# The first layer's output projection: one column block of four in seven block products for eight

## The chip, the cores and the metric

The kernel runs on one core of one Trainium2 chip. The metric is the device time of one execution in microseconds (us). Three runs of the kernel before took 1990.0, 1988.53 and 1989.0 us, with a median of 1989.0.

The engines are called by the profile's names: PE (TensorE, matrix products), PEld (its weight loads), DVE (VectorE), ACT (ScalarE), POOL (GpSimd), SP (SyncE, which here only issues DMAs).

## The reference

A trunk of two layers over 256 tokens of width 2048, in float32. What matters here is the first layer:

```python
n = rms_norm(h, attn_norm[i])
z = n @ a_w_in[j]
...
mix = neighbourhood_attention(q, k, v, a_rpb[j])
cross = memory_attention(qm, km, vm)
h = h + jnp.concatenate([mix, cross], axis=-1) @ w_o[i]
n = rms_norm(h, mlp_norm[i])
h = h + jnp.square(jax.nn.relu(n @ w_up[i])) @ w_down[i]
```

The change concerns the product with `w_o[0]`.

## The kernel before, in words

**Precision.** Each float32 operand of a product is split into a high part (rounded to the type that PE reads, `fp32r`) and a low part (the difference). A product is three matmuls: high by high, high by low, low by high, summed in PSUM. `split` (L506) makes the parts: a copy on ACT, then a subtraction on DVE.

**The attention output.** It lies in `cat` (L901 and after): 16 contraction tiles of 128 partitions, each with 256 high and 256 low columns, one column for each token. Head `hd` gives tile `hd`, the four memory heads the tiles 12 to 15. `attend3` (L682) writes a tile, the last one some five grains after the last key projection (`a_k_done`, L891).

**The output projection.** `add_o` (L1021) cuts the 2048 result columns into four blocks of 512, and each block's weights into four chunks of 1 MB (four contraction tiles by 512 columns). Blocks 0 and 1 are worked alternately, with the chunks in the order 3, 0, 1, 2, since the last heads are ready last; then block 2, then block 3, chunks 0 to 3 each. A chunk is a `Work` of two halves (`halves_of`, L252); a half is a "grain", the unit in which `run_all` (L446) walks through the program. A grain of the projection multiplies two contraction tiles: 2 tiles x 2 halves of the tokens x 3 matmuls, a 128x128 piece of `cat` as the stationary operand and 512 weight columns as the moving one (`m_products`, L379). Blocks 0 and 1 are grains 0 to 15, block 2 grains 16 to 23, block 3 grains 24 to 31.

**Ahead of a grain.** `ahead(n)` in `run_all` writes out, before grain n's products, the preparation of later ones: loads, "lift", "pre" and "prep", each by its own distance (`Grain`, L154). For the projection, "prep" issues the chunk's load on SP's queue into a ring of three places (`raw`, L274), and splits half a chunk into one of four places for high and low parts (`new_half`, L353; the split at L508 and L509). `later(n, ...)` puts a step n grains off. `past` (L933) makes a step come after a given pair of split instructions. The framework's planner then orders each engine's instructions by a modelled time and inserts the waits; an engine's queue runs in that order.

**PSUM.** Eight banks: four under the tag `acc`, which the sums of the blocks take by twos, two under `att`, and one pair `two` for the attention scores.

**After a block.** `o_done` (L939) adds a block's two sums to the residual `h` on DVE (L988) and sums squares on ACT (L922). After block 0 it also closes attention's scratch pool `work` and opens `side` in the same memory. After block 2, `guard` (L942) takes the mean square of three blocks as a provisional scale; blocks 0, 1 and 2 are scaled (L964), transposed in 32x32 blocks on DVE and by DMA (`far_blocks`, L620), and split into `hT` (`arrived`, L634; L538 and L539). Block 3 follows the same way (L1009). The true root mean square is put in later, by `inv` (L972). The MLP's first products (`up_grains`, L1055) read `hT`; three of them leave the last quarter of the contraction, which comes from block 3, for after one another's first three quarters (L1111).

**Where the method of the change already is.** The MLP's second product works on 2x2 blocks with seven products for eight. `down_grains` (L1176) copies a block of weights (L1198) and has POOL issue an accumulating DMA that adds another (L1199), adds three more sums on DVE (L1205 to L1207), and splits both parts; `squared` (L1133) makes the sums of the left operand. The lists `FIRST` and `SECOND` name each product with its left and right block:

```python
FIRST = ("p3", 6, 0), ("p1", 0, 1), ("p2", 2, 2)
SECOND = ("p7", 4, 0), ("p6", 5, 1), ("p4", 1, 2), ("p5", 3, 3)
```

p2, p3 and p4 go to one result block each; p1, p5, p6 and p7 are shared and folded by additions afterwards.

Of the kernel before, what the change touches and what calls it, by code (L numbers as in the profile page):

```python
# [10 lines left out]
F32 = mybir.dt.float32  # L11
# [6 lines left out]
P = 128  # L18
# [24 lines left out]
STEPPED = [sum(n for x, n in RUNS if x == q) for q in range(2)]  # L43

REST = (2, 0, 1, 3)
GUARD = 3

MOVING_AT = 160

# [101 lines left out]
class Grain:  # L151


    def __init__(self, run, after=None, load=None, pre=None, prep=None, ahead=(8, 5, 3), lift=None):  # L154
        self.run, self.after, self.stages = run, after, (load, lift, pre, prep)
        self.ahead = ahead[0], 8, *ahead[1:]


@with_exitstack
def encoder_kernel(ctx: ExitStack, tc: tile.TileContext, t: dict, out: bass.AP):  # L160
# [206 lines left out]
    def later(n, fn, *args):  # L367
        pending.append((state["tick"] + n, fn, args))
# [116 lines left out]
    def parts_of(name):  # L485

        return lambda k, i: tuple(box[name][:, k, b * SEQ + i * P : b * SEQ + (i + 1) * P] for b in range(2))
# [18 lines left out]
    def split(dst_hi, dst_lo, src):  # L506

        first = nc.scalar.activation(dst_hi, src, AF.Copy)  # L508
        return first, nc.vector.tensor_tensor(dst_lo, src, dst_hi.bitcast(F32), op=ALU.subtract)  # L509
# [40 lines left out]
    def summed(ps, name, row, factor=1.0):  # L550

        s = at.work.tile([P, SEQ], F32, tag="sum_s", name=f"{name}_s")
        nc.vector.scalar_tensor_tensor(s, ps, factor, row, op0=ALU.mult, op1=ALU.mult)
        return s
# [157 lines left out]
    def attention(jobs, at, gap=1, steps=(0, 1, 3, 4), rest=0):  # L712


        def step(n, job, prev):
            qT, kT, bias, v, head, cat = job
            if n == 0:
                res = attend(qT, kT, bias)
                box["scaled", head] = box["scaled"]
            elif n == 1 and len(steps) == 4:  # L720
                res = turned(prev)
            elif n < len(steps) - 1:
                res, box["pT", head] = halved(prev) if len(steps) == 4 else attend2(prev)
            else:
                if "between" not in box:
                    return attend3(prev, v, head, cat)
                with tc.issue_after(box.pop("between").ins):
                    return attend3(prev, v, head, cat)
            results[n, head] = res

        results = {}
        for t in range(len(jobs) + len(steps) - 1):
            for n in range(len(steps)):
                if 0 <= t - n < len(jobs):
                    j = t - n
                    more = rest if n == len(steps) - 1 and j == len(jobs) - 1 else 0
                    later(at + gap * j + steps[n] + more,
                          lambda n=n, job=jobs[j]: step(n, job, results.get((n - 1, job[4]))))
# [20 lines left out]
    def head_of(v, hd):  # L759
        return lambda part, kt: v[:, part, kt, hd * HD : (hd + 1) * HD]  # L760
# [130 lines left out]
    def a_k_done(hd):  # L891
        def f(w):
            k = at.work.tile([P, 512], F32R, tag="b_y2", name="kT")
            s = summed(w.ps, "k", box["x_row"])
            split(k[:, :SEQ], k[:, SEQ:], s)
            b = at.work.tile([P, (ROWS + 2) * GRID_W], F32, tag="b_o", bufs=3, name="bias")
            nc.sync.dma_start(b[:, : NT * NEAR], t["bias"][hd])
            attention([(box.pop(("q", hd)), k, b, head_of(box["v", hd // GH], hd % GH), hd, box["cat"])], 1)
        return f

    def a_qm_done(hd):  # L901
# [23 lines left out]
    def mean_square(which, n, name):  # L925

        s = small.tile([P, NT], F32, tag="ss0", name="ss_t")
        nc.vector.tensor_reduce(s, ssq[which][:, :, :n], axis=AX.X, op=ALU.add)
        v = keep.tile([P, NT], F32, tag=name, name=name)
        nc.vector.tensor_scalar(v, s, 1.0 / (n * 512), EPS, op0=ALU.mult, op1=ALU.add)  # L930
        return v
# [7 lines left out]
    def o_done(layer, nb):  # L939
        which = 2 * layer  # L940

        def guard():  # L942

            box["near"] = mean_square(which, GUARD, "near")
            box["scale"] = keep.tile([P, NT], F32, tag="scale", name="scale")
            nc.gpsimd.tensor_tensor(box["scale"], box["near"], mhalf[:, :NT], op=ALU.pow)
            box["hT"] = shifted(f"hT{layer}")

        def begun():

            y = at.side.tile([P, NT, 512], F32, tag="T", bufs=2, name="h_s")
            for i in range(NT):
                nc.scalar.activation(y[:, i, :], h[:, i, D - 512 :], AF.Copy, scale=box["scale"][:, i : i + 1])
            box["begun"] = y

        def scaled(b):

            if b < 2:
                box["room", b] = at.side.tile([P, 2, 1024], F32, tag="b", bufs=3, name="h_t")
                y = box["room", b][:, 0]  # L960
            else:
                y = at.side.tile([P, 1024], F32, tag="T", bufs=2, name="h_s")
            for i in range(NT):
                nc.scalar.activation(y[:, i * 512 : (i + 1) * 512], h[:, i, b * 512 : (b + 1) * 512], AF.Copy,  # L964
                                     scale=box["scale"][:, i : i + 1])
            box["raw", b] = far_blocks(lambda i: y[:, i * 512 : (i + 1) * 512], (box["room", b % 2][:, 1], y))
            box["still"] = y

        def landed(b):
            arrived(box["hT"], box["raw", b], b * 4, (G_M0, G_M1)[layer])  # L970

        def inv():  # L972

            v = mean_square(which, 4, "full")
            box["inv"] = keep.tile([P, NT], F32, tag="inv", name="inv")
            nc.vector.reciprocal(v, v)
            nc.vector.tensor_tensor(box["inv"], v, box["near"], op=ALU.mult)
            box["ninv"] = keep.tile([P, NT], F32, tag="ninv", name="ninv")
            nc.vector.tensor_scalar(box["ninv"], box["inv"], -1.0, None, op0=ALU.mult)

        def f(w):
            if nb == 0:
                closed("work")
                at.side = opened("side", side="right")
            def add():
                for i in range(NT):
                    hs = h[:, i, nb * 512 : (nb + 1) * 512]
                    added = nc.vector.tensor_tensor(hs, w.ps[i], hs, op=ALU.add)  # L988
                if nb == 0:
                    box["added"] = added  # L990

            def squares():
                for i in range(NT):
                    sum_squares(which, i, nb)

            if nb < 3:
                add()
                squares()
            if nb == GUARD - 1:
                later(1, guard)  # L1000
                for n, fn, *args in ((2, scaled, 0), (3, scaled, 1), (4, scaled, 2), (4, landed, 0), (5, landed, 1),
                                     (7, landed, 2), (7, begun)):

                    later(n, lambda fn=fn, args=args: past(lambda: fn(*args), box["weights"]))
            if nb == 3:
                y = box["begun"]

                def summed(i):
                    nc.vector.scalar_tensor_tensor(y[:, i, :], w.ps[i], box["scale"][:, i : i + 1], y[:, i, :],  # L1009
                                                   op0=ALU.mult, op1=ALU.add)  # L1010
                    return y[:, i, :]

                raw = far_blocks(summed, (box["still"], y.rearrange("p t c -> p (t c)")))
                box["summed"] = box["turned"]
                box["ready"] = arrived(box["hT"], raw, 12, (G_M0, G_M1)[layer])
                later(8, past, add)
                later(10, past, squares)
                later(12, lambda: past(inv, box["both", 1]))
        return f

    def add_o(layer):  # L1021
        first, second, third, late = 3, 0, 1, 2
        for n in (0, 2):
            if n:
                order = [(b, c) for b in range(2) for c in range(4)]
            else:
                order = [(b, c) for b in range(2) for c in (first, second)]
                order += [(b, c) for c in (third, late) for b in range(2)]
            add_ms([([t[f"w_o{layer}"][nb * 4 + c] for c in range(4)], o_done(layer, nb)) for nb in (n, n + 1)],
                   parts_of("cat"), order)  # L1030
            if layer and n == 0:
                plan[-1].behind = plan[-2].behind = plan[-1].last_block = True

# [830 lines left out]
```

## Time and profile before

| what | before |
|---|---|
| median of three runs | 1989.0 us (1988.53 to 1990.0) |
| the profiled execution | 1989.6 us |
| its span in the profile | 1987.8 us |
| granted clock of PE | 0.999 |
| DVE, ACT, POOL busy | 87%, 73%, 8% of the span |
| read from HBM | 397.78 MB, 202 GB/s over the span |

The span runs from the first to the last instruction on the chip; 1.8 us of the execution lie around it. A row of the timeline reads: start in the span, length, engine, line, operation, `out<-in`, the tile (for a matmul stationary x moving), the count, and in brackets how long the engine sat idle before it and what ended that. Matmuls are pipelined: the length of one is a latency, and the next one starts before it ends. PEld works beside PE. Busy times of a stretch are sums for each engine, so engines overlap in them.

### The profile page before, as it was taken

The page shows a single profiled execution, that of the slowest core. Times are in us where ns is not written, and L with a number is a line of the kernel's source. Part 1 is how long each engine was busy: PE and PEld are TensorE (multiplying, and loading weights), DVE is VectorE, ACT ScalarE, POOL GpSimd, SP SyncE. Part 2 cuts the span into 40 slices and gives each one's busy share as a digit, 9 for nine tenths or more (in the row PEclk, how much of TensorE's full clock was granted, in tenths as well). Part 3 has the DMA queues.
Part 4 walks back from the last instruction along what each step waited for, and adds up shares of the span by engine and source line. Part 5 has one row for each costly group of instructions (what it writes and reads, how often), then busy time and mean ns, then how long its engine had stood idle before and what let it go on. Part 6 is the DMA issues. An engine that isn't in the chain of part 4 may idle for free.

```text
span 1987.8 us, 33096 instructions
## 1 busy us (share of the span) xinstructions
PE 1977.8 (99%) x12816; PEld 1796.3 (90%) x12816; DVE 1729.1 (87%) x2098; ACT 1443.7 (73%) x2109; POOL 152.6 (8%) x205
## 2 busy tenths in 40 slices
PE   9999999999999999999999999999999999999998
PEld 8999999899999999999998888889999999999997
DVE  6777777589999999999999879789999999999997
ACT  6755555478887878777887657668788777877786
POOL 0000000000000000000001001001000000000001
PEclk9999999999999999999999999999999999999999
DMA  7856555768777777777778765668777777777775
GB/s 289 319 193 209 199 193 184 267 210 258 218 231 236 229 230 239 225 241 232 223 228 222 269 221 172 218 205 260 239 225 227 236 230 229 237 229 241 228 227 157
DMA packets 112862, 453.51 MB, mean 228 GB/s; under 512 B 19009, under 2 KB 42689, under 8 KB 65345
## 3 DMA queue, kind: packets, MB, share of 16 engines
q1 hardware_dynamic: 92320, 414.43, 61.1%
q0 software_dynamic: 20096, 36.45, 10.4%
q8 instruction: 100, 1.64, 0.3%
q10 hardware_dynamic: 288, 0.52, 0.1%
q14 instruction: 58, 0.47, 0.1%
HBM read 397.78 MB, written 4.19 MB: 202 GB/s over the span
## 4 chain that ended last, share of the span: by engine, by line
PE 98%; DVE 1%; issue 0%; DMA 0%; ACT 0%; SPq 0%; POOL 0%; DVEq 0%; POOLq 0%; ACTq 0%
PE ps_u L411 35%; PE ps_s L411 10%; PE p L1231 10%; PE p L1235 10%; PE p L1234 10%; PE ps_m L391 7%; PE ps_m L392 7%; PE ps_m L388 7%; DMA raw<-in_w_first 0%; PE sc_ps L605 0%; PE sc_ps L604 0%; PE sc_ps L606 0%; PE av L698 0%; PE av L699 0%; PE av L700 0%
## 5 line engine op out<-in xcount | busy, mean ns | idle before, releaser
L411 PE MATMUL ps_u<-hT,uh 128*128 128x256 f32 x3812 | 662.5, 276 | 0.0
L411 PEld LDWEIGHTS ps_u<-hT,uh 128*128 128x128 f32 x3812 | 578.7, 188 | 5.7
L411 PE MATMUL ps_u<-hT,ul 128*128 128x256 f32 x1964 | 542.6, 276 | 0.0
L508 ACT ACTIVATE uh<-raw_U 128x1024 fp32r<-128x1024 f32 x258 | 273.5, 1061 | 154.0 <-PE ps_u L411 151.6
L411 PEld LDWEIGHTS ps_u<-hT,ul 128*128 128x128 f32 x1964 | 368.7, 188 | 0.0
L508 ACT ACTIVATE hi<-raw 128x1024 fp32r<-128x1024 f32 (+1 forms) x215 | 222.1, 1037 | 183.0 <-PE ps_m L392 93.1
L509 DVE TENSOR_TENSOR lo<-raw,hi 128x1024 fp32r<-128x1024 f32 (+1 forms) x215 | 255.0, 1191 | 108.0 <-ACT hi L508 107.2
L509 DVE TENSOR_TENSOR ul<-raw_U,uh 128x1024 fp32r<-128x1024 f32 x258 | 314.2, 1219 | 9.2 <-ACT uh L508 9.2
L509 DVE TENSOR_TENSOR tl<-t,th 128x2048 fp32r<-128x2048 f32 x120 | 274.8, 2290 | 51.4 <-ACT th L508 51.1
L508 ACT ACTIVATE th<-t 128x2048 fp32r<-128x2048 f32 x120 | 231.0, 1925 | 91.3 <-PE p L1235 91.3
L509 DVE TENSOR_TENSOR bl<-b,bh 128x1536 fp32r<-128x1536 f32 x120 | 210.2, 1752 | 0.0
L1199 POOL DMA_DIRECT2D t<-b x120 | 104.4, 870 | 1156.9 <-ACT t L1198 1097.2
L1231 PE MATMUL p<-th,a_s 128*128 128x512 f32 x480 | 187.5, 391 | 0.0
L1234 PE MATMUL p<-tl,a_s 128*128 128x512 f32 x480 | 187.2, 390 | 0.0
L1235 PE MATMUL p<-th,a_s 128*128 128x512 f32 x480 | 186.7, 389 | 0.0
L508 ACT ACTIVATE bh<-b 128x1536 fp32r<-128x1536 f32 x120 | 178.8, 1490 | 3.5
L411 PE MATMUL ps_s<-nT,hi 128*128 128x256 f32 x896 | 154.6, 277 | 0.0
L1235 PE MATMUL p<-bh,a_s 128*128 128x512 f32 x360 | 140.9, 391 | 0.0
L1234 PE MATMUL p<-bl,a_s 128*128 128x512 f32 x360 | 140.1, 389 | 0.0
L1231 PE MATMUL p<-bh,a_s 128*128 128x512 f32 x360 | 140.1, 389 | 0.0
L411 PEld LDWEIGHTS ps_s<-nT,hi 128*128 128x128 f32 x896 | 135.3, 188 | 0.2
L411 PE MATMUL ps_s<-nT,lo 128*128 128x256 f32 x448 | 124.2, 277 | 0.0
(298 smaller groups left out, 3669.2 us busy)
## 6 DMA issues: line engine op xcount, KB each, us to landing
raw_U<-in_w_up SPq DMA_DIRECT2D x128, 1024.0 KB, 6.4
b<-in_w_pair SPq DMA_DIRECT2D x120, 1024.0 KB, 5.8
raw<-in_w_o SPq DMA_DIRECT2D x32, 1024.0 KB, 5.0
t<-b POOLq DMA_DIRECT2D x120, 256.0 KB, 6.6
raw<-in_w_b SPq DMA_DIRECT2D x21, 1024.0 KB, 5.4
raw<-in_w_av SPq DMA_DIRECT2D x12, 1024.0 KB, 5.0
raw<-in_w_aq SPq DMA_DIRECT2D x12, 1024.0 KB, 4.9
raw<-in_w_ak SPq DMA_DIRECT2D x12, 1024.0 KB, 4.8
```

The costliest lines, as they stand in the source:

```text
L388: first = nc.tensor.matmul(ps, ah, hi[:, s], start=st, stop=False)
L391: nc.tensor.matmul(ps, ah, lo[:, s], start=False, stop=False)
L392: final = nc.tensor.matmul(ps, al, hi[:, s], start=False, stop=sp)
L411: ins = nc.tensor.matmul(ps, x, acts[:, k, part], start=k == n == 0, stop=k == KT - 1 and n == 2)
L508: first = nc.scalar.activation(dst_hi, src, AF.Copy)
L509: return first, nc.vector.tensor_tensor(dst_lo, src, dst_hi.bitcast(F32), op=ALU.subtract)
L1199: nc.gpsimd.dma_start(s[:, 3, :], b[:, 1, :], accum_op=ALU.add)
L1231: ins = nc.tensor.matmul(ps, a[:, 0, ai, :], hi[:, s], start=entered, stop=False, skip_group_check=True)
L1234: nc.tensor.matmul(ps, a[:, 0, ai, :], lo[:, s], start=False, stop=False, skip_group_check=True)
L1235: nc.tensor.matmul(ps, a[:, 1, ai, :], hi[:, s], start=False, stop=ends, skip_group_check=True)
```

## The change

Block 2 of the first layer's projection (columns 1024 to 1535) is worked in another way for three of its four chunks, 3, 0 and 1; chunk 2 stays as it was and goes first. In each half of the three chunks, two contraction tiles, two halves of the tokens and two halves of the columns (256 each) make 2x2 blocks, and seven products of blocks take the place of eight: 21 matmuls over 256 columns for 12 over 512, in each of six grains. The grains keep their number and places.

- `sums_ahead`, called after the last key head, makes the sums of the left operand for six pairs of contraction tiles: ACT copies the high parts of `cat`, POOL issues an accumulating DMA of the low parts, DVE makes four sums, and they are split. They are spread over ticks 1 to 12. The scratch has two places in a tile of attention's pool; the results take the place of `nT`.
- `half(...)` prepares a grain: the load of a chunk (first of its two grains), an ACT copy of 256 columns with an accumulating DMA from POOL (two places, `s_x`), three DVE additions, and two splits, 768 columns into the ring's places and 1024 into `t_x` (three places).
- The sums lie in the two `att` banks and the pair `two`; block 3 takes `acc` as before.
- `fold` copies the shared sums out of PSUM, combines them by four subtractions of 256 columns, and adds all to `h`.
- The provisional scale of the first layer is taken from two blocks; the second layer's stays at three.
- The weights of the three chunks are reordered on the host: the four blocks of a half as 3, 0, 2, 1.

```diff
-GUARD = 3
+GUARDS = 2, 3
+CROSSED = (3, 0, 1)
+CROSSED_NB = 2
...
     def a_k_done(hd):
...
+            box["last_k"] = split(k[:, :SEQ], k[:, SEQ:], s)
...
+            if hd == NH - 1:
+                sums_ahead()
...
          def f(w):
...
-            if nb < 3:
+            if layer == 0 and nb == CROSSED_NB:
+                w.fold()
+                squares()
+            elif nb < 3:
                 add()
                 squares()
-            if nb == GUARD - 1:
+            if nb == 2:
                 later(1, guard)
...
+    def sums_ahead():
+        pairs = [4 * c + 2 * hf for c in CROSSED for hf in range(2)]
+        room = at.work.tile([P, 2, 8, P], F32, tag="l4", name="c_x")
+        box["crossed"] = keep.tile([P, len(pairs), 2, 4, P], F32R, tag="wide", name="a_x")
+        def together(n):
+            k, c = pairs[n], room[:, n % 2, :4].rearrange("p (k b) j -> p k (b j)", k=2)
+            both = box["cat"][:, k : k + 2, :].bitcast(F32)
+            nc.scalar.activation(c, both[:, :, :SEQ], AF.Copy)
+            nc.gpsimd.dma_start(c, both[:, :, SEQ:], accum_op=ALU.add)
+        def summed(n):
+            c, a = room[:, n % 2], box["crossed"][:, n]
+            nc.vector.tensor_tensor(c[:, 4, :], c[:, 0, :], c[:, 2, :], op=ALU.subtract)
+            nc.vector.tensor_tensor(c[:, 5:7, :], c[:, 0:8:4, :], c[:, None, 1, :].to_broadcast([P, 2, P]), op=ALU.add)
+            nc.vector.tensor_tensor(c[:, 7, :], c[:, 3, :], c[:, 6, :], op=ALU.subtract)
+            past(lambda: split(a[:, 0], a[:, 1], c[:, 4:]), box["last_k"])
+        for n in range(len(pairs)):
+            at_tick = max(2 * n, 1)
+            later(at_tick, together, n)
+            later(at_tick + 2, summed, n)
...
+        def fold():
+            z = at.side.tile([P, 4, SEQ], F32, tag="T", bufs=2, name="z_x")
+            hs = [h[:, i, nb * 512 : (nb + 1) * 512] for i in range(NT)]
+            for n in range(2):
+                nc.scalar.activation(z[:, 2 * n : 2 * n + 2].rearrange("p a b -> p (a b)"), sums["two"][:, n, :], AF.Copy)
+            for i in range(NT):
+                nc.vector.tensor_tensor(hs[i], sums["direct"][i], hs[i], op=ALU.add)
+            for d, x, y in ((1, 1, 0), (2, 1, 2), (1, 1, 3), (3, 3, 2)):
+                nc.vector.tensor_tensor(z[:, d], z[:, x], z[:, y], op=ALU.subtract)
+            for n, i in enumerate((1, 0)):
+                nc.vector.tensor_tensor(hs[i], z[:, 2 * n : 2 * n + 2].rearrange("p a b -> p (a b)"), hs[i], op=ALU.add)
+        def half(n, c, hf):
...
+            def lift():
+                b, s = blocks(), at.side.tile([P, 4, SEQ], F32, tag="T", bufs=2, name="s_x")
+                own["s"] = s
+                nc.scalar.activation(s[:, 3], b[:, 3], AF.Copy)
+                nc.gpsimd.dma_start(s[:, 3], b[:, 1], accum_op=ALU.add)
+            def pre():
+                b, s = blocks(), own["s"]
+                nc.vector.tensor_tensor(s[:, 0], b[:, 3], b[:, 0], op=ALU.add)
+                nc.vector.tensor_tensor(s[:, 1], s[:, 0], b[:, 1], op=ALU.add)
+                nc.vector.tensor_tensor(s[:, 2], s[:, 1], b[:, 2], op=ALU.add)
+            def prep():
+                own["b"] = [x[:, : 3 * SEQ] for x in new_half("M")]
+                box["weights"] = split(*own["b"], blocks()[:, :3].rearrange("p a b -> p (a b)"))
+                room = at.side.tile([P, 2, HALF], F32R, tag="b", bufs=3, name="t_x")
+                own["t"] = room[:, 0], room[:, 1]
+                split(*own["t"], own["s"].rearrange("p a b -> p (a b)"))
+            def run():
...
+                for products, (bh, bl) in ((FIRST, own["b"]), (SECOND, own["t"])):
+                    for name, ai, bi in products:
...
+                            own[name] = nc.tensor.matmul(ps, ah, bh[:, s], start=st, stop=False, skip_group_check=True)
+                        nc.tensor.matmul(ps, ah, bl[:, s], start=False, stop=False, skip_group_check=True)
+                        nc.tensor.matmul(ps, al, bh[:, s], start=False, stop=last, skip_group_check=True)
...
+            g = Grain(run, after, load if hf == 0 else None, pre, prep, lift=lift)
+            g.ahead = 6, 5, 4, 3
...
+            works = [([t[f"w_o{layer}"][nb * 4 + c] for c in range(4)], o_done(layer, nb)) for nb in (n, n + 1)]
+            if n and layer == 0:
+                crossed_works(o_done(0, CROSSED_NB))
+                works, order = works[1:], [(0, c) for c in range(4)]
```

## Prediction before the run

> **What bounds the kernel now.** I read the page first, then the tensor engine's rows in order of time around the first layer's output projection, then busy time by stage, and last the rows at the seam to the MLP.
>
> ```profile
> span 1987.8 us, 33096 instructions
> ## 1 busy us (share of the span) xinstructions
> PE 1977.8 (99%) x12816; PEld 1796.3 (90%) x12816; DVE 1729.1 (87%) x2098; ACT 1443.7 (73%) x2109; POOL 152.6 (8%) x205
> ...
> PE 98%; DVE 1%; issue 0%; DMA 0%; ACT 0%; SPq 0%; POOL 0%; DVEq 0%; POOLq 0%; ACTq 0%
> ```
>
> PE is busy for 99% of the span and makes up 98% of the chain that ended last. So work taken from PE is worth its full length, if PE stays fed. "Busy" is modelled, so I look at start times:
>
> ```profile
> 319.79 0.39 PE L411 MATMUL ps_s<-nT,hi 128*128 128x256 f32 x2
> ...
> 323.19 0.40 PE L411 MATMUL ps_s<-nT,hi 128*128 128x256 f32 x2
> ```
>
> ```profile
> 375.63 0.39 PE L388 MATMUL ps_m<-hi,cat 128*128 128x512 f32 x1
> ...
> 397.39 0.39 PE L388 MATMUL ps_m<-hi,cat 128*128 128x512 f32 x1
> ```
>
> Between the first two rows lie 30 matmuls over 256 columns (ten groups of two hi and one lo): 3.40 / 30 = 0.1133 us each. Between the second two lies the whole third block, 96 matmuls over 512 columns: 21.76 / 96 = 0.2267 us each. The "0.39" of a row is a latency; the spacing counts. Half the columns cost half the time to the last digit, although the narrow ones change their stationary tile every time too.
>
> ```profile
> 332.00:361.00 29.00, 29.00 (x134) 24.19 (x133) 17.44 (x26) 13.65 (x20) 0.00 (x0) 1.00 0.59 203
> 361.00:395.00 34.00, 34.00 (x152) 28.15 (x151) 20.18 (x19) 17.34 (x23) 0.00 (x0) 1.00 0.71 265
> 395.00:419.00 24.00, 24.00 (x108) 19.87 (x107) 19.15 (x26) 17.13 (x29) 0.71 (x1) 1.00 0.46 111
> ```
>
> Columns: stretch, length, then busy us of PE, weight load, DVE, ACT and POOL, the granted clock (1.00), DMA share. The stretches are blocks 0 and 1, the end of block 1 with block 2, and block 3. PE has no hole; DVE has 11.6, 13.8 and 4.9 us free, ACT 15.4, 16.7 and 6.9.
>
> **The change part by part.** *PE.* A pair of contraction tiles costs 2 tiles x 2 token halves x 3 = 12 matmuls of 512 columns, 12 x 0.2267 = 2.72 us (one grain). Seven products of 3 matmuls over 256 columns cost 21 x 0.1133 = 2.38 us. Six pairs save 6 x 0.34 = **2.04 us**, a tenth of a percent. The unchanged two grains run from 375.63 to 381.07, the six from there to 395.35, where block 2 ended at 397.39. No PE wait in the trace ends in this stage, so nothing else can be won here.
>
> The rows give no fixed cost of a matmul. [...]
>
> *Preparation of a grain.* Before: one ACT copy and one DVE subtraction over 1024 columns. After: an ACT copy of 256, an accumulating DMA from POOL, three DVE additions of 256, and two splits, of 768 and 1024.
>
> ```profile
> 382.36 1.23 DVE L509 TENSOR_TENSOR lo<-raw,hi 128x1024 fp32r<-128x1024 f32 x1 [1.49 <-ACT hi L508]
> ...
> 436.48 0.28 DVE L1149 TENSOR_TENSOR c<-c 128x128 f32<-128x128 f32 x1
> 436.80 0.42 DVE L1150 TENSOR_TENSOR c<-c 128x256 f32<-128x256 f32 x1
> ...
> 440.14 0.68 DVE L1205 TENSOR_TENSOR t<-b 128x512 f32<-128x512 f32 x1
> ```
>
> ```profile
> 328.72 0.40 ACT L508 ACTIVATE cat<-av_s 128x256 fp32r<-128x256 f32 x1
> ...
> 389.43 1.06 ACT L508 ACTIVATE hi<-raw 128x1024 fp32r<-128x1024 f32 x1 [1.66 <-PE ps_m L392]
> ```
>
> 768 columns lie between 512 and 1024: 0.95 us on DVE, and on ACT, between 256 and 1024, 0.85. DVE: 3 x 0.42 + 0.95 + 1.23 = 3.44 us a grain, ACT: 0.40 + 0.85 + 1.06 = 2.31, PE 2.38. So during the six grains **DVE is slower than PE**, by 6.4 us in all; only work done ahead can hide that. From 361 to two microseconds before the new end (393.35, the same end less 2.04) DVE would need 20.18 - 6 x 1.23 + 6 x 3.44 = 33.4 us of 32.35: 1.1 too many. ACT needs 17.34 - 6 x 1.06 + 6 x 2.31 = 24.8 and fits. What covers DVE is the lead of today's splits: the row at 382.36 ends at 383.59 and serves the grain that starts at 389.23 (five of 2.72 after 375.63), so 5.6 us can be eaten before PE feels it. If that cover were gone, the whole 1.1 would be PE's.
>
> *Sums of the left operand.* Six pairs, at ticks 1 to 12 after the last key head, so beside blocks 0 and 1: DVE 0.28 + 0.42 + 0.28 + 0.68 = 1.66, ACT two passes of 512, by the 256 and 1024 rows about 0.6 each. DVE takes 10.0 us of the 11.6 free in the first stretch, ACT 7.2 of 15.4: hidden, with 1.6 us to spare on DVE; without that, up to 10 us would be pushed into the stretch above. The accumulating DMA stands in POOL's queue behind the memsets of the last heads, which has cost nobody there, as the sums aren't read before 381.07.
>
> *The accumulating DMA and its two places.*
>
> ```profile
> raw<-in_w_o SPq DMA_DIRECT2D x32, 1024.0 KB, 5.0
> t<-b POOLq DMA_DIRECT2D x120, 256.0 KB, 6.6
> ```
>
> ```profile
> L1199 POOL DMA_DIRECT2D t<-b x120: 862/872/963, 431.8 to 1933.7; - x120
> ...
> DMA to landing us min/median/max: 3.2/6.6/10.8
> ```
>
> No 128 KB accumulation is in the trace; the same operation at 256 KB lands after 3.2 to 10.8 us. The sum tiles `s_x` have two places, their splits `t_x` three. The tightest chain I find is that of the sixth grain: `t_x` of the fourth needs the place of the first (free at 381.07 + 2.38 = 383.45), its split takes 1.06 + 1.23 = 2.29, then the sixth may be copied (0.40), issued (0.87), landed (L) and split (2.29): ready at 389.30 + L. PE reads it in the second half of that grain, 381.07 + 5 x 2.38 + 9 x 0.1133 = 393.99. So L up to 4.7 us is free; 6.6 makes PE late by 1.9, 10.8 by 6.1. Half the bytes should lie between the fastest and the median row; I take 5.0, **0.3 us late**. The weight loads on SP stay sixteen of the same size, now asked for some grains earlier:
>
> ```profile
> 355.84 0.33 SPq L274 DMA_DIRECT2D raw<-in_w_o  x1
> ```
>
> That place in the ring of three now takes the first changed chunk: landed at 355.84 + 5.0 = 360.8, twenty microseconds before use. Nothing else on SP waits for it.
>
> *Fold and seam.* At block 2's end come two ACT copies out of PSUM, four DVE subtractions of 256 and two more additions of 512: DVE 4 x 0.42 + 2 x 0.68 = 3.04 us beyond before, in block 3's stretch with 4.9 free, of which 1.8 are left.
>
> ```profile
> 418.84 1.69 DVE L539 SCALAR_TENSOR_TENSOR hT<-h_s,first,hT 128x256 fp32r<-128x256 f32 x4 [1.28 <-ACT hT L538]
> 420.44 0.75 DVE L1009 SCALAR_TENSOR_TENSOR h_s<-ps_m,scale,h_s 128x512 f32<-128x512 f32 x1
> ...
> 429.86 1.67 DVE L539 SCALAR_TENSOR_TENSOR hT<-h_s,first,hT 128x256 fp32r<-128x256 f32 x4
> ```
>
> ```profile
> 431.31 0.30 PEld L411 LDWEIGHTS ps_u<-hT,uh 128*128 128x128 f32 x2
> ```
>
> The last quarter of `hT` is started by DVE at 420.44, its first tile is split at 429.86 + 1.67 / 4 = 430.3, and PE reads it at 431.31: 1.0 us of slack. A backlog of DVE beyond 1.8 + 1.0 = 2.8 us reaches PE here. The guard helps: it sums two blocks now, so scaling of the first two need not wait for block 2. Backlog by the terms above runs from 1.1 to 5.6 us (the lead that may be eaten), late by 0 to 2.8; I take **0.9**, nearer to the low end.
>
> *Sum.* -2.04 + 0.3 + 0.9 = -0.8 us. The profiled execution took 1989.6 (span 1987.8 and 1.8 around it); it becomes 1988.8. The median of the runs is 0.6 lower, 1989.0, so the forecast in its terms is 1988.2.
>
> **The rivals.** *Full gain.* Every accumulation lands within 4.7 us and the seam keeps its slack: 1989.0 - 2.04 = 1987.0. For it: the 3.2 us row and PE's unbroken rate. Against: DVE is 99% booked from 332 to 393 (17.44 + 10.0 + 33.4 = 60.8 of 61.35).
>
> *DVE and the two places become the bound: slower.* `s_x` and `t_x` lie in the room that attention leaves, and the sums' scratch now lives there until the last of them. Two pairs go at a time: copy 0.6, issue 0.87, landing, sums 0.98, split 1.3. From 332, with 5.0 us of landing, three rounds of 8.8 end at 358, ahead of the first chunk; with 10.8, three of 14.6 end at 376. If the first copy comes only at 374, three rounds of 0.40 + 0.87 + 5.0 + 2.29 = 8.6 end at 399.8 instead of 393.99, 5.8 late, and the seam adds 0.9 to 2.8: 1989.0 - 2.04 + 7.6 = 1994.6. It decides from a first copy at about 373 on: then PE has lost over 6 us. Against it: POOL's 120 issues never took over 0.96 us, and DMA has room (share 0.59) in that stretch.
>
> *The gain is not there.* Were a narrow matmul held up by its weight load (0.19 us a row, overlapped), seven products would cost what eight did: 1989.0 plus the 1.2 of stalls, 1990.2. The 0.1133 spacing speaks against it, and the operands here have the same shapes.
>
> **How the numbers follow.** Forecast, with stalls up to 3 us: 0.45; full gain 0.25; slower rival 0.2; no gain 0.1. "Within 0.2%" is 1985.0 to 1993.0, about what a measurement of this kernel can tell from no change. Even a full gain stays inside, so faster gets 0.04, for a better order elsewhere; slower 0.21, the rival and some ends of the unknown landing. The range runs from full gain less the spread of the runs shown (1 us), 1986.0, to the latest landing, 1989.0 - 2.04 + 6.1 + 0.9 = 1994.0, which leaves out the worse half of the rival.
>
> **What would show it.** Right: narrow matmuls 0.113 apart in block 2, its end near 395.7, the stage from 361 nearly full on DVE, and the last `hT` read within a microsecond of its split. Wrong: holes in PE's starts before the fifth or sixth grain (landing over 4.7 us), a first `s_x` copy after 370, a spacing over 0.12, or PE waiting at the first MLP products for longer than 3 us.

## The result and the profile after

The changed kernel takes 1999.35 us, the median of six runs (1998.51 to 2000.78), beside 1989.27 us (1988.53 to 1990.0) for the kernel before in as many runs. The ratio is 1.0052 with a 95% interval of 1.0039 to 1.0065: **slower by half a percent**, 10 us. The forecast of 1988.2 us and its range up to 1994.0 us are both missed.

The head of the page of the changed kernel:

```profile
span 1998.2 us, 33317 instructions
...
PE 1980.2 (99%) x12870; PEld 1800.5 (90%) x12870; DVE 1749.9 (88%) x2152; ACT 1457.5 (73%) x2135; POOL 164.4 (8%) x217
...
PE 95%; DVE 2%; DMA 1%; ACT 1%; issue 1%; SPq 0%; DVEq 0%; POOL 0%; POOLq 0%; ACTq 0%
```

The span grew by 10.4 us, PE's busy time by 2.4. So most of the loss is not work: PE's share of the chain that ended last fell from 98% to 95%, and DVE, DMA, ACT and issue took what it left. The view of what PE waited for says where. The columns are the waiting instruction, what released it, the total in us, how often, and the longest. First the changed kernel, then the kernel before:

```profile
PE ps_u L415 <- ACT hT L542: 5.1, 2, 3.7
PE ps_u L415 <- DVE hT L543: 2.1, 1, 2.1
```

```profile
PE idle L240 <- POOL mhalf L234: 1.0, 1, 1.0
```

The longest before was the microsecond on `mhalf` at the kernel's start, which both have. New are 7.2 us on `hT`, the left operand of the MLP's first product. PE's rows in order of time, the changed kernel:

```profile
383.20 0.28 PE L1128 MATMUL ps_m<-hi,a_x 128*128 128x256 f32 x1
...
385.70 0.28 PE L1128 MATMUL ps_m<-hi,a_x 128*128 128x256 f32 x1
...
417.61 0.40 PE L415 MATMUL ps_u<-hT,uh 128*128 128x256 f32 x2
...
436.55 0.38 PE L415 MATMUL ps_u<-hT,uh 128*128 128x256 f32 x1 [3.73 <-ACT hT L542]
439.03 0.58 PE L415 MATMUL ps_u<-hT,uh 128*128 128x256 f32 x1 [2.10 <-DVE hT L543]
...
441.02 0.41 PE L415 MATMUL ps_u<-hT,uh 128*128 128x256 f32 x1
...
443.58 0.41 PE L415 MATMUL ps_u<-hT,uh 128*128 128x256 f32 x1
...
451.42 0.40 PE L1357 MATMUL p<-bh,a_s 128*128 128x512 f32 x1
```

and the kernel before:

```profile
419.15 0.40 PE L411 MATMUL ps_u<-hT,uh 128*128 128x256 f32 x2
...
441.10 0.40 PE L1231 MATMUL p<-bh,a_s 128*128 128x512 f32 x1
```

The projection ends 1.54 us earlier (417.61 for 419.15). From there to the first matmul of the MLP's second product lie 33.81 us (451.42 - 417.61) where there were 21.95 (441.10 - 419.15): 11.86 us lost, 10.3 in all. **Everything is gained inside the projection and lost at the seam behind it.** Busy time by stretch in the changed kernel; the columns are those of the prediction:

```profile
361.00:395.00 34.00, 34.00 (x199) 30.21 (x198) 29.87 (x44) 23.76 (x35) 6.41 (x7) 1.00 0.80 269
395.00:419.00 24.00, 24.00 (x125) 20.40 (x124) 23.30 (x32) 16.57 (x28) 0.00 (x0) 1.00 0.58 178
419.00:430.00 11.00, 8.75 (x75) 8.36 (x74) 7.19 (x9) 4.56 (x7) 0.00 (x0) 1.00 0.43 80
430.00:440.00 10.00, 4.18 (x30) 3.78 (x30) 4.99 (x8) 4.43 (x8) 0.86 (x1) 0.89 0.98 388
440.00:445.00 5.00, 5.00 (x26) 4.96 (x25) 1.97 (x4) 1.31 (x4) 0.00 (x0) 0.53 1.00 347
```

PE is full to 419. From 419 to 440 it stands still for 2.25 + 5.82 = 8.1 us, and in the last row the granted clock is 0.53. There 12 matmuls take 2.56 us (441.02 to 443.58), 0.213 each where 0.1133 is usual. Counted from start to start, the four holes are 1.67, 1.13, 4.00 and 2.48 us long; less one usual spacing each they cost 8.8. The 26 matmuls from 439.03 to 444.79 lie too far apart and cost another 2.8. Together that is 11.6 of the 11.9. In the ten microseconds from 430, where PE stands longest, DVE is busy for 4.99 and ACT for 4.43: what PE waits for is not a shortage of an engine but something that comes late. Followed back, it is one chain. The changed kernel, ACT's and DVE's rows:

```profile
405.57 0.45 DVE L1079 TENSOR_TENSOR z_x<-z_x 128x256 f32<-128x256 f32 x1
...
412.92 0.68 DVE L1081 TENSOR_TENSOR first<-z_x,first 128x512 f32<-128x512 f32 x1
...
415.06 2.09 DVE L631 STREAM_TRANSPOSE h_t<-h_s 128x512 f32<-128x512 f32 x2
...
422.02 1.71 ACT L542 ACTIVATE hT<-h_s,first 128x256 fp32r<-128x256 f32 x4 [5.19 <-DMA h_s<-h_t]
422.56 1.69 DVE L543 SCALAR_TENSOR_TENSOR hT<-h_s,first,hT 128x256 fp32r<-128x256 f32 x4 [3.93 <-ACT hT L542]
424.28 2.13 DVE L631 STREAM_TRANSPOSE h_s<-h_s 128x512 f32<-128x512 f32 x2
```

The kernel before, the same steps:

```profile
397.10 1.28 DVE L988 TENSOR_TENSOR first<-ps_m,first 128x512 f32<-128x512 f32 x2
...
410.06 2.09 DVE L627 STREAM_TRANSPOSE h_t<-h_s 128x512 f32<-128x512 f32 x2 [1.15 <-DMA h_t<-h_t]
...
418.29 1.71 ACT L538 ACTIVATE hT<-h_s,first 128x256 fp32r<-128x256 f32 x4 [2.76 <-DMA h_s<-h_t]
...
421.22 1.09 DVE L627 STREAM_TRANSPOSE h_s<-h_s 128x512 f32<-128x512 f32 x1
```

Block 2's last sum ends at 413.6 (412.92 + 0.68) instead of 398.4. The fold's subtractions and additions are strewn over eight microseconds, between splits and `hT` tiles in DVE's queue. So block 2 is transposed 5.0 us later (415.06 for 410.06) and the third quarter of `hT` split 3.7 later (422.02 for 418.29). And block 3's transposition writes into the room from which that third quarter is read (`box["still"]`, in `far_blocks`' second argument): it can't start before 424.25 and comes 3.1 us later (424.28 for 421.22). Then SP's queue and ACT's. The changed kernel:

```profile
426.44 1.27 SPq L634 DMA_DIRECT2D h_s<-h_s  x2
427.75 0.60 SPq L1178 DMA_DIRECT2D raw_U<-in_w_up  x1
428.39 1.27 SPq L634 DMA_DIRECT2D h_s<-h_s  x2
...
434.09 2.00 ACT L512 ACTIVATE u_z<-raw_U 128x1024 fp32r<-128x1024 f32 x2 [7.51 <-DMA raw_U<-in_w_up]
436.00 1.69 ACT L542 ACTIVATE hT<-h_s,first 128x256 fp32r<-128x256 f32 x4
```

The kernel before:

```profile
424.13 2.60 SPq L630 DMA_DIRECT2D h_s<-h_s  x4
426.78 0.61 SPq L1052 DMA_DIRECT2D raw_U<-in_w_up  x1
...
429.23 1.71 ACT L538 ACTIVATE hT<-h_s,first 128x256 fp32r<-128x256 f32 x4 [4.28 <-DMA h_s<-h_s]
...
432.50 2.02 ACT L508 ACTIVATE u_z<-raw_U 128x1024 fp32r<-128x1024 f32 x2 [0.72 <-DMA raw_U<-in_w_up]
```

**Two queues have changed their order.** Before, SP issued the four pieces of block 3's transposition and then the load `raw_U` of 1 MB; now the load stands between the second and the third piece. Before, ACT split the last quarter of `hT` and then `u_z`; now `u_z` stands ahead and waits 7.51 us for that very load. The last quarter, issued 2.3 us later (426.44 for 424.13), is split 6.8 us later (436.00 for 429.23). None of the lines that changed touches this load or this split.

### The profile page after: what moved, and what is told of

Its sections match the earlier page's. It is cut to its first block, busy times and chain, and to the rows that moved or that the text cites. A ratio compares the mean times of both kernels' runs of the same rounds, so it can differ in the third digit from the quotient of the medians.

```text
span 1998.2 us, 33317 instructions
## 1 busy us (share of the span) xinstructions
PE 1980.2 (99%) x12870; PEld 1800.5 (90%) x12870; DVE 1749.9 (88%) x2152; ACT 1457.5 (73%) x2135; POOL 164.4 (8%) x217
## 4 chain that ended last, share of the span: by engine, by line
PE 95%; DVE 2%; DMA 1%; ACT 1%; issue 1%; SPq 0%; DVEq 0%; POOL 0%; POOLq 0%; ACTq 0%
PE ps_u L415 34%; PE p L1357 10%; PE p L1361 10%; PE p L1360 10%; PE ps_s L415 9%; PE ps_m L395 7%; PE ps_m L396 7%; PE ps_m L392 7%; DMA first<-in_x 0%; DVE nT L543 0%; DMA h_s<-h_s 0%; SPq L634 0%; DVE hT L543 0%; PE sc_ps L608 0%; PE sc_ps L610 0%
## 5 line engine op out<-in xcount | busy, mean ns | idle before, releaser
L512 ACT ACTIVATE hi<-raw 128x1024 fp32r<-128x1024 f32 (+2 forms) x215 | 220.5, 1031 | 157.1 <-PE ps_m L396 72.3
L513 DVE TENSOR_TENSOR lo<-raw,hi 128x1024 fp32r<-128x1024 f32 (+2 forms) x215 | 253.2, 1183 | 80.6 <-ACT hi L512 80.0
L513 DVE TENSOR_TENSOR ul<-raw_U,uh 128x1024 fp32r<-128x1024 f32 x258 | 314.5, 1220 | 10.4 <-ACT uh L512 10.4
```

## The experiments

The theories go by letters. **F**: the fold makes block 2's last sum late. **P**: the preparation of the six grains (DVE's load, the accumulating DMAs) does. **G**: the guard over two blocks is itself the harm. **Q**: the changed order of the two queues carries the loss. **A**: the spacing of the narrow matmuls (0.119 us, below) comes from where their operands lie.

**Taking the fold out, and putting it on the kernel before.** The first kernel drops the fold's copies, subtractions and last additions:

```diff
         def fold():
-            z = at.side.tile([P, 4, SEQ], F32, tag="T", bufs=2, name="z_x")
...
-            for n in range(2):
-                nc.scalar.activation(z[:, 2 * n : 2 * n + 2]..., sums["two"][:, n, :], AF.Copy)
             for i in range(NT):
                 nc.vector.tensor_tensor(hs[i], sums["direct"][i], hs[i], op=ALU.add)
-            for d, x, y in ((1, 1, 0), (2, 1, 2), (1, 1, 3), (3, 3, 2)):
-                nc.vector.tensor_tensor(z[:, d], z[:, x], z[:, y], op=ALU.subtract)
-            for n, i in enumerate((1, 0)):
-                nc.vector.tensor_tensor(hs[i], z[...], hs[i], op=ALU.add)
```

> The changed kernel without the shared sums: p1, p5, p6 and p7 are computed but never copied out of PSUM nor added to the residual, so block 2 lacks them; the two direct additions stay. Theory F (the fold's eight extra operations, strewn over a booked DVE queue, hold up block 2's last sum, and through it hT): the last sum comes some 9 us earlier, hT no longer holds PE, 1987 to 1989 us. Theory P (the sixth grain's operand, prepared late in two places, ends block 2 at 401.3 instead of 395.4, and that alone makes hT late): block 2 still ends near 401, PE still waits, 1993 us or more.

Measured: 1990.4 us (1988.3 to 1992.35), ratio 1.0007 (0.9996 to 1.0018): the loss is all but gone, though the time lies a little above what F had, with the whole preparation in place, and the four pieces are issued together again. Block 2's products end even later there: the last one starts at 403.05, in the changed kernel at 401.28. The second is the kernel before with the fold's ten operations (two copies, four subtractions, two more additions beside its two) behind its plain block 2:

```diff
+            if layer == 0 and nb == 2:
+                z = at.side.tile([P, 4, SEQ], F32, tag="T", bufs=2, name="z_x")
...
+                for n in range(2):
+                    nc.scalar.activation(z[...], w.ps[n], AF.Copy)
+                add()
+                for d, x, y in ((1, 1, 0), (2, 1, 2), (1, 1, 3), (3, 3, 2)):
+                    nc.vector.tensor_tensor(z[:, d], z[:, x], z[:, y], op=ALU.subtract)
+                for n, i in enumerate((1, 0)):
+                    nc.vector.tensor_tensor(hs[i], z[...], hs[i], op=ALU.add)
+                squares()
```

> The kernel before with only the fold's operations added at the end of its plain block 2 (two ACT copies of its sums, four DVE subtractions of 256, two more additions of 512; they change block 2's values). No product, no preparation and no guard of the change. F: the block ends at 397.4 as before, but its last sum comes up to 10 us later and PE waits for hT: 1994 to 1999 us. P: a block that ends on time leaves room for the fold: 1989 to 1990.5 us.

Measured: 1999.86 us (1999.36 to 2000.14), ratio 1.0052 (1.0029 to 1.0075). **The fold alone costs as much as the whole change**, without one narrow matmul and without preparation (its guard is over three blocks still, of which more below). Its rows:

```profile
402.13 0.68 DVE L1005 TENSOR_TENSOR first<-z_x,first 128x512 f32<-128x512 f32 x1
...
426.76 1.27 SPq L630 DMA_DIRECT2D h_s<-h_s  x2
428.08 0.60 SPq L1063 DMA_DIRECT2D raw_U<-in_w_up  x1
...
434.07 2.00 ACT L508 ACTIVATE u_z<-raw_U 128x1024 fp32r<-128x1024 f32 x2 [7.19 <-DMA raw_U<-in_w_up]
435.98 1.69 ACT L538 ACTIVATE hT<-h_s,first 128x256 fp32r<-128x256 f32 x4
```

Here the last sum ends only 4.4 us later (402.13 + 0.68 for 397.10 + 1.28), and the same two orders have turned. So P is not needed for the turn: it comes without the preparation, and with the preparation but no fold it stays away.

**Less preparation, and the guard as it was.** One chunk of the three is kept in the new form, so two grains are prepared for six; and the guard is set back to three blocks:

```diff
-CROSSED = (3, 0, 1)
+CROSSED = (3,)
```

> The changed kernel with one chunk of three in seven products (two grains, 6 matmuls of 256 columns fewer, 0.68 us), so that the preparation is light and its two places do; fold and guard as in the change. F: the fold is whole, so most of the loss stays: 1994 us or more. P: block 2 ends on time, 1988 to 1990 us.

```diff
-GUARDS = 2, 3
+GUARDS = 3, 3
```

> The changed kernel with the provisional scale taken from three blocks again. F and P: scaling blocks 0 and 1 now waits for the late block 2 as well, so it is no faster than the change: 1999 us or more. A third theory G (the early scale lets transposes and splits of blocks 0 and 1 go ahead of the fold on DVE): the fold goes first, 1990 to 1996 us.

Measured: two grains 1999.34 us (1998.81 to 1999.67), ratio 1.0051 (1.0032 to 1.0071), no better than six. With the guard of three 2006.18 us (2005.66 to 2006.69, two runs), ratio 1.0083 (1.0054 to 1.0113): the early guard is worth 6.8 us (2006.18 - 1999.35), and G falls. It also sets the comparison above right. With a guard of three blocks in both, the change costs 6.3 us more than the fold alone (2006.18 - 1999.86). So the rest of the change is not free, the early guard pays for it, and that the two medians near 1999.5 agree is partly chance. The kernel with two grains tells more than its time:

```profile
424.50 1.93 SPq L634 DMA_DIRECT2D h_s<-h_s  x3
426.52 0.55 SPq L1178 DMA_DIRECT2D raw_U<-in_w_up  x1
427.12 0.61 SPq L634 DMA_DIRECT2D h_s<-h_s  x1
```

Its pieces begin at 424.50, 0.4 us later than in the kernel before, and still ACT splits the last quarter of `hT` only at 435.51, 6.3 us later than 429.23. One piece of four behind the load is enough. That speaks for Q over a mere lateness.

**The fold earlier.** The six new grains go first and the plain chunk last, in two banks of its own, so that the fold may run beside the plain chunk's products:

```diff
-        for n, c in enumerate(plain):
-            plan.append(Work("M", ..., begin, lambda w: None))
...
         plan.extend(half(2 * n + hf, c, hf) for n, c in enumerate(CROSSED) for hf in range(2))
+        for n, c in enumerate(plain):
+            plan.append(Work("M", ..., plain_begin, plain_done if n == len(plain) - 1 else None))
```

> The changed kernel with the six grains first and the plain chunk last, in banks of its own: the shared sums and the direct ones are folded while the plain chunk runs (one DVE addition of 512 more in all), so that only two additions stand behind block 2's end, as before the change. Theory F (the fold behind block 2 is what makes hT late, its length alone counts): 1987 to 1990 us. Theory Q (the fold is only the push: what costs is that the planner, its modelled times moved, lets a weight load stand between the pieces of block 3's transposition on SP, and the fourth weight column's split, which waits for that load, ahead of hT's last quarter on ACT): the built queues have that order here too, 1993 us or more.

Measured: 1999.23 us (1998.32 to 2000.13, two runs), ratio 1.005 (1.003 to 1.007). Nothing gained: the load still stands between the pieces. But the fold did not come early either. In DVE's queue its last addition starts at 409.74, and block 2's last sum ends at 414.7 (413.6 in the changed kernel). What F needed did not come about, so this run does not decide between F and Q.

**Holding the orders.** In the changed kernel the load of the MLP's fourth weight block is told to follow the last piece of the transposition (and is written out two grains later, 6 for 8 ahead), and the splits of that block to follow `hT`'s:

```diff
-            nc.sync.dma_start(raw[:, :, a].rearrange("p t k j -> p t (k j)"),
+            box["piece"] = nc.sync.dma_start(raw[:, :, a].rearrange("p t k j -> p t (k j)"),
...
-            own["raw"] = loaded(t[f"w_up{layer}"][m], "U")
+            with tc.issue_after(box["piece"].ins) if m == 3 and layer == 0 else nullcontext():
+                own["raw"] = loaded(t[f"w_up{layer}"][m], "U")
...
+            if m == 3 and layer == 0:
+                past(lambda: prepared(hf), box["ready"])
+                return
...
-        return [Grain(..., early if m < 2 else SOONER),
+        return [Grain(..., early if m < 2 else (6, 8, 4) if m == 3 and layer == 0 else SOONER),
```

> The changed kernel with two orders held by hand: the fourth weight column's load after the last piece of block 3's transposition on SP, and its splits after hT's last quarter on ACT and DVE. Q: hT's last quarter lands some 3 us after its last piece instead of 6 and isn't held by the split, 4 to 7 us come back, 1992 to 1995 us. F: the fold is as late as before, and with it all of hT: 1998 us or more.

The same edit on the plain block with the fold, on the version with the plain chunk last, and on the kernel before, as a control:

> The kernel before with the fold's operations behind its plain block 2 (block 2's values change) and the two orders held. Against the same without them, 1999.9 us. Q: 1990 to 1994 us. F: within 1 us of 1999.9.

> The changed kernel with the plain chunk last and both orders held. F and Q both: neither the fold nor the queues hold hT, the saved 2.04 us show: 1986.9 to 1988.5 us. If preparation in two places (theory P), which now has 5.4 us less lead, costs PE: 1989 us or more.

> The kernel before with both orders held, which are those that it has anyway. All theories: 1989.1 us within 0.7; a change here would be the price or the gain of holding the orders themselves.

Measured: 1993.06 us (1991.63 to 1994.68), ratio 1.0019 (1.0008 to 1.0029), for the changed kernel; 1992.65 (1991.83 to 1994.18), 1.0018 (1.0007 to 1.0028), for the plain block with the fold; 1991.76 (1991.15 to 1992.9), 1.0014 (1.0005 to 1.0024), with the plain chunk last, which misses what F and Q had and lies where P had it; 1989.19 (1988.55 to 1990.33), 1.0001 (0.9992 to 1.0011), for the control. **The order carries 6.3 us of the changed kernel's loss** (1999.35 - 1993.06) and 7.2 of the fold's on the plain block (1999.86 - 1992.65), and to hold it costs nothing by itself. The changed kernel with both orders held, PE's waits and one stretch:

```profile
PE ps_u L415 <- ACT hT L542: 1.1, 1, 1.1
...
PE ps_u L415 <- DVE hT L543: 0.9, 2, 0.5
```

```profile
430.00:440.00 10.00, 9.13 (x75) 8.59 (x74) 7.97 (x15) 7.12 (x13) 0.86 (x1) 1.00 0.99 345
```

The waits on `hT` fall from 7.2 to 2.0 us, and the clock stays at 1.00 where it had begun to fall (0.89). So the 6.3 us are not lateness alone: the last quarter of `hT` is split 3.9 us earlier (432.11 for 436.00), and the 2.8 us of the matmuls that lay too far apart are gone too.

**Which of the two orders?** Only the order of the splits is held, on ACT and with it on DVE; SP is left free:

```diff
+            if m == 3 and layer == 0:
+                past(lambda: prepared(hf), box["ready"])
+                return
```

> The changed kernel with only ScalarE's order held: the splits of the fourth weight block of the MLP wait until the last quarter of hT is split. The load on SP's queue is free to come between the pieces of the last transposition, as in the changed kernel. Holding both orders gave 1993.1 us; which of the two carried the 6.3 us is asked. If the split that stands ahead on ScalarE is the cost (S): ScalarE starts the last quarter of hT at 432 to 433 us in the span as with both held, no half clock, and 1993 to 1994 us. If the load between the pieces is the cost (L): the pieces issued behind it land up to 6.1 us after their issue at 428.4 to 429.7, so the quarter starts at 434.5 to 435.5 instead of 436.0, PE's hole stays near 3 us, and the time is 1997 to 1999 us. Each about half: near 1995.5.

Measured: 1998.84 us (1997.27 to 2000.94), ratio 1.0049 (1.0035 to 1.0063). L was right:

```profile
428.20 0.60 SPq L1178 DMA_DIRECT2D raw_U<-in_w_up  x1
428.84 1.27 SPq L634 DMA_DIRECT2D h_s<-h_s  x2
...
435.29 1.71 ACT L542 ACTIVATE hT<-h_s,first 128x256 fp32r<-128x256 f32 x4 [8.29 <-DMA h_s<-h_s]
```

ACT is now idle for 8.29 us with nothing ahead of `hT`, and what it waits for is the pieces themselves. **The load on SP is what delays them**; ACT's split in front only hid it. The starts of all runs, from SP's, ACT's and PE's rows, make one table (the last two are explained below it). "From issue" is the last quarter's first split less the issue of the first of its four pieces:

| kernel | last four pieces | order on SP | last quarter of `hT` on ACT | from issue | first matmul of the second product | median |
|---|---|---|---|---|---|---|
| before | 424.13 | four, load | 429.23 | 5.1 | 441.10 | 1989.3 |
| before, orders held | 424.23 | four, load | 429.50 | 5.3 | 441.36 | 1989.2 |
| no shared fold | 424.52 | four, load | 429.96 | 5.4 | 441.73 | 1990.4 |
| changed, orders held | 426.82 | four, load | 432.11 | 5.3 | 444.45 | 1993.1 |
| fold on plain, held | 427.53 | four, load | 432.82 | 5.3 | 445.16 | 1992.7 |
| plain chunk last, held | 425.13 | four, load | 430.50 | 5.4 | 442.83 | 1991.8 |
| changed | 426.44 | two, load, two | 436.00 | 9.6 | 451.42 | 1999.4 |
| fold on plain | 426.76 | two, load, two | 435.98 | 9.2 | 451.67 | 1999.9 |
| two grains | 424.50 | three, load, one | 435.51 | 11.0 | 450.56 | 1999.3 |
| plain chunk last | 426.50 | two, load, two | 435.43 | 8.9 | 451.12 | 1999.2 |
| split order held | 426.89 | two, load, two | 435.29 | 8.4 | 450.46 | 1998.8 |
| guard of three | 430.54 | two, load, two | 442.50 | 12.0 | 457.33 | 2006.2 |
| two grains, plain chunks last, held | 421.36 | four, load | 426.65 | 5.3 | 440.50 | 1989.9 |
| plain chunk last, held, operands moved | 426.76 | four, load | 431.91 | 5.1 | 444.35 | 1992.4 |

With the pieces together the split follows 5.1 to 5.4 us after the first issue in every kernel; with the load among them, 8.4 to 12.0.

**What is left with the orders held.** The best version, plain chunk last and both orders held, was run with one chunk for three:

> The changed kernel with the plain chunks last, both orders held and only one chunk (two grains) in seven products. If DVE's load from the preparation is what still holds hT in the version with three chunks (1991.8 us): little of it is left, 1988.3 to 1989.5 us. If the fold and the two-block guard alone do it: 1990.5 us or more.

Measured: 1989.86 us (1988.7 to 1991.65), ratio 1.0004 (0.9994 to 1.0014), a little above what was expected; no wait on `hT` is left in PE's list. The step from six grains to two gives 1.9 us back, though four grains' saving on PE goes with them. Whether those 1.9 us are the preparation's or the fold's this run does not separate: with two grains three plain chunks follow the fold, and its last addition ends before 395 instead of at 409.0, so both are lighter or earlier at once. PE's longest wait with six grains:

```profile
PE ps_u L415 <- DVE ul L513: 1.4, 1, 1.4
```

It is a wait for DVE, which was busy for 31.71 of 34 us in the stretch from 361 (25.94 with two grains, 20.18 in the kernel before). No version tried is measurably faster than the kernel before.

**The spacing.** In the same version the weight parts and the left operand's sums were moved by 160 bytes within their rows, to where other operands of the kernel lie:

```diff
-                own["b"] = [x[:, : 3 * SEQ] for x in new_half("M")]
+                own["b"] = [at.ring.tile([P, HALF + n], F32R, tag=x, bufs=4, name=x)[:, MOVING_AT // 4 :][:, : 3 * SEQ]
+                            for x, n in LONGER.items()]
...
-        box["crossed"] = keep.tile([P, len(pairs), 2, 4, P], F32R, tag="wide", name="a_x")
+        wide_x = keep.tile([P, KT * 512 + P], F32R, tag="wide", name="a_x")
+        box["crossed"] = wide_x[:, MOVING_AT // 4 :][...]
```

> The changed kernel with the plain chunk last and both orders held, and two operands moved by 160 bytes in their tiles: the first split of each grain (moving, in p1, p2 and p3) and the sums of the left operand (stationary, in p3, p5, p6 and p7). The narrow matmuls of the change start 0.119 us apart, those of the projections 0.1133. Theory A (a moving and a stationary operand that begin at the same place of a row get in each other's way): p1, p2, p5, p6 and p7, whose two operands now differ by 160 bytes, go at 0.113, p3 and p4 stay at 0.119; the time falls by 0.5 us against 1991.8. Theory B (it is the products' own: changing sums every three matmuls): all stay at 0.119 and the time at 1991.8.

Measured: 1992.43 us (1991.59 to 1994.56), ratio 1.0018 (1.0008 to 1.0029), and still about 0.119 us from one narrow matmul to the next. A falls for this shift; why they are slower here than elsewhere stays open.

## Why the prediction was wrong, point by point

**The bound: right.** PE is full through both blocks (34.00 of 34.00 us from 361 and 24.00 of 24.00 from 395), and the time is PE's plus PE's holes.

**PE's saving: right mechanism, size too large.** Seven products of one grain start at 383.20 and the next grain's at 385.70: 2.50 / 21 = 0.119 us, not the 0.1133 of the rows I took from the attention. A grain saves 2.72 - 2.50 = 0.22 us, six of them 1.3 instead of 2.04; at the end of block 3 the trace is 1.54 ahead, of which 0.35 were there at the projection's first matmul (330.04 for 330.39), so 1.2.

**The preparation on DVE: right in direction.** I had DVE short by 1.1 us in the stretch from 361; it was busy for 29.87 of the 34.00 (20.18 before), and not the bound there, but what it does was done late.

**The sixth grain's operand: later than I said, and free for PE.** First the issues and landings of the accumulating DMA, then the split of the last `t_x`:

```profile
L1098 POOL DMA_DIRECT2D s_x<-raw x6: 856/884/1084, 361.2 to 388.0; - x6
...
DMA to landing us min/median/max: 3.5/5.4/9.3
```

```profile
396.51 1.22 DVE L513 TENSOR_TENSOR t_x<-s_x,t_x 128x1024 fp32r<-128x1024 f32 x1
```

The median landing of 5.4 us bears out the 5.0 I took. The last operand is ready at 397.73, 3.7 us behind the 393.99 at which I had it read, where I said 0.3. PE lost nothing by it: the planner had put matmuls of block 3 in between. But so block 2's last product starts only at 401.28, where I had the block end at 395.35, and that lateness went on into the fold, where I didn't follow it.

**The fold and the seam: this is the step that failed.** I took the fold as 3.04 us out of 4.9 that DVE had free, set the 1.8 left and 1.0 of slack (2.8 us) against a backlog of 1.1 to 5.6, and wrote "late by 0 to 2.8; I take 0.9". At the seam 11.9 us were lost. Three things were wrong in it. It asked how much DVE had to do, not what waited for the last of it: the additions stand at the head of scaling, transposition and split, and through the shared room also of block 3's transposition. The cover was read at the last quarter of `hT` alone, as if only DVE's backlog could make it late; its DMAs were in no term. And I took the order of the queues as given, although the planner orders by modelled times and the change moves those. With the orders held the seam is late by the first of these: in the fold on the plain block by 3.6 us (1992.65 for 1989.09, the kernel before measured beside it). The turned order adds 6.3 to 7.5 us (three kernels with and without it); nothing in my sum stood for it.

**The guard: right.** I gave it no size; it is worth 6.8 us, and the change would have cost 0.8% without it.

**The rivals.** The slower one had the right sign and a time of 1994.6, but not the mechanism: it decides by a first `s_x` copy after 373 us, and POOL's first issue is at 361.2. That the narrow matmuls give nothing at all did not hold either. Of the signs that I had named for being wrong, one came up: PE waited at the first MLP products for longer than 3 us, namely 7.2.

What I did not settle: which modelled time turned SP's order. The trace shows the order, not the planner's reasons; only that adding the fold turns it and that taking the fold out, or holding the load, turns it back. Nor is the rest of the loss, 4.0 us in the changed kernel with the orders held, divided between fold and preparation.

## What to carry to other kernels

Before pricing an addition on an engine that is not the bound, follow what waits for its *last* instruction, through the rooms that are shared too, to the next thing the bound engine reads. Where a planner orders the queues, work added in one place can let a large load slip in among small urgent transfers in another; look in both traces at the order on the DMA queue around the seam first, and pin the order where it matters (here free: 1.0001, 0.9992 to 1.0011). Weigh that against the prize: the most that this change could win was a tenth of a percent.

## What the runs showed of the hardware

**A load among small transfers.** The issue-to-landing times of the transposition pieces that are written to `h_s` on SP between 405 and 440 us, minimum, median and maximum of eight issues (four of block 2, four of block 3). The changed kernel, and the changed kernel with both orders held:

```profile
DMA to landing us min/median/max: 2.7/2.8/6.1
```

```profile
DMA to landing us min/median/max: 2.7/2.8/3.2
```

The load of 1 MB issued between them takes the slowest from 3.2 to 6.1 us. In the changed kernel the load, issued at 427.75, lands at 434.1; the two pieces behind it, issued at 428.39 and 429.04, land at 434.5 and 434.9, and the two ahead of it took 2.7 and 3.0 us. Both pieces behind the load land after it, within 1 us. What held them until then these traces do not show.

**Half a clock after a hole.** PE's idle time of 3.73 us before 436.55 and the 2.10 on DVE's `hT` behind it were followed by a granted clock of 0.53 over 440 to 445. That is a mean: from 440 to 443 the clock is 0.50, and there matmuls start 0.213 us apart. With only the order of the splits held the longest wait was 2.56 us and the clock from 440 to 445 was 0.56; with both orders held the longest wait on `hT` was 1.1 us and the clock stayed at 1.00. In the changed kernel the clock was still 1.00 over 436 to 437, 0.93 over 437 to 438 and 0.50 over 438 to 439: it fell in the second hole, not in that of 3.73 us. With the order of the splits held, the same followed a shorter wait, the 2.56 us with two small ones of 0.22 and 0.38 us behind it. With two grains, orders not held, the clock was 0.93 over 431 to 434 and 0.50 over 434 to 437. A step from 1.00 to 0.50 with that mean lies, by my estimate, between 433 and 434, at most 3.1 us into a hole that began at 430.9. How long a hole must be for the clock to fall these runs do not show.
